# RWKV-7 time mixing in a two-layer hybrid: centred value rows, unsplit decay sums, the bonus moved to forward rounds, and another order between the states' steps

## Chip, cores and metric

The kernel runs on one core of one Trainium2 chip. The metric is the device time of one execution in microseconds (us); the time before is the median of three runs. Below, PE is TensorE (matmul), DVE is VectorE, ACT is ScalarE, POOL is GpSimd and SP is SyncE, which issues DMA transfers.

## What is computed

A backbone of two layers over 1024 latent tokens of width 1024, with 256 context tokens ahead. The first layer is attention; the second is bidirectional RWKV-7 time mixing beside a long convolution, and its output goes through a projection, a residual sum and a final norm. The change lies in the RWKV-7 part, eight heads of width 64, in two directions:

```python
def wkv_scan(s0, r, decay, k, v, kk, b, reverse, emit):
    def step(s, inp):
        r_t, w_t, k_t, v_t, kk_t, b_t = inp
        sa = jnp.einsum('bhij,bhj->bhi', s, kk_t)
        s = s * w_t[:, :, None, :] - sa[..., None] * b_t[:, :, None, :] + v_t[..., None] * k_t[:, :, None, :]
        y = jnp.einsum('bhij,bhj->bhi', s, r_t) if emit else None
        return s, y
...
def rwkv_readout(y, r, k_bonus, v, r_k, gn_w, gn_b):
    mean = jnp.mean(yf, axis=-1, keepdims=True)
    var = jnp.mean(jnp.square(yf - mean), axis=-1, keepdims=True)
    yn = ((yf - mean) * lax.rsqrt(var + RWKV_GN_EPS)).reshape(y.shape[:2] + (BRANCH_W,))
    yn = (yn * gn_w + gn_b).astype(v.dtype)
    bonus = jnp.sum(r * k_bonus * r_k, axis=-1, keepdims=True) * v
    return yn + bonus.reshape(yn.shape)
```

The readout's y is the sum over both directions. A row of the state has one value channel; y's mean over these channels is linear in the value rows.

## The kernel before

The scan is done in chunks. A **job** is a pair of heads j (four of them) in one direction d, forward (d = 0) before backward; a **unit** is 256 tokens of a job, the first of the five being the context (q = 0). So there are 8 x 5 = 40 units. `rwkv` runs nine of the units' first parts ahead, and then 45 rounds, `rw_round(b)` for b = -4 to 40. One round works on many units at different stages:

- `rw_next_load` and `rw_cast` (unit b + 14): the inputs of a front; the cast splits the decay logits `sg` into two parts `sgs` (ACT rounds, GpSimd takes the remainder) and makes `kd` and `af`.
- `rw_front` (unit b + 13): running sums of the decay, `cs_ps`, by products with a triangular matrix; exponentials on ACT; scaled keys `AKR`, `kd`, `BK` on DVE.
- `rw_turned`, `rw_gram` (the front of the round before): transposes (`bk_ps`), 16 small products `g_ps` of keys with keys, masked on DVE into `LG`; the diagonal 32x32 blocks go to DRAM (`LD`).
- `rw_invert`: for a whole job those blocks come back as `L` (80 blocks side by side, on 80 partitions), and 31 steps of forward substitution on DVE make their inverses X. A step is two instructions, tmp = L times X and X = X minus tmp. `PACE` says how many steps a round takes at each of three places: 2, 1 and 6. The first one is at the end of the round in which the job's last front is ready. The inverses go through DRAM (`XD`) to `XT`.
- `rw_keys_turned`, `rw_right` (unit b + 4): the right sides `rh_ps`, copied to R by ACT; `rw_first` (b + 3, `y_ps`), `rw_blocks`, `rw_second` (b + 2, `z_ps`, DVE takes it off R) and `rw_solved` (b + 1, `w_ps`): block substitution.
- `rw_trans` (b + 1): `ph_ps`, from which DVE makes PH and RT; `rw_own` (b + 1): the unit's own share `sy_ps` from UV.
- `rw_scan` (unit b): four steps, each PH times the state S, S again through ACT, and RT times S for the output.
- In a backward round with q > 0, `rw_bonus` loads six arrays and makes the bonus factor (GpSimd and DVE); a round later `rw_stats` subtracts the mean `gmu`, takes the variance `gvr` and scales Y, `rw_readout` does the bonus product `bo_ps`, the transposition `yt_ps`, the affine part and the gate, and `rw_split` splits the result for the projection.
- From round 28 on, `Final` loads, scales and splits the weights of the projection, and from round 31 projects row blocks (`fe_ps`) by the table `PLAN`, at the end of a round.

Inside the rounds PE, DVE, ACT and GpSimd keep the program's order (`nc.ordered(True)`); the order of SP's transfers is set by the scheduler. PSUM tiles of tag "f" share four banks in turn, so a product can wait until an older tile has been read: `rh_ps` comes to the bank of `z_ps`.

```python
for b in range(-4, 41):
    self.rw_round(b)
```

Of the kernel before, what the change touches and what calls it, by code (L numbers as in the profile page):

```python
# [29 lines left out]
def constants():  # L30
# [5 lines left out]
    c["k_ones2"] = b  # L36
    p = np.zeros((128, 128), np.float32)
# [90 lines left out]
PACE = (5, 2, 1, 6)  # L128
# [68 lines left out]
class K:  # L197
# [1064 lines left out]
    def rw_init(self):  # L1262
# [13 lines left out]
        tri = fp.tile([128, 3, 256], F32, name="tri0", tag="kkr", bufs=2)  # L1276
        nc.sync.dma_start(out=tri[:, 0:2], in_=a["k_tri"].rearrange("d p k -> p d k"))
        C["tri"] = fp.tile([128, 2, 256], F32R, name="tri", bufs=1)
        nc.vector.tensor_copy(out=C["tri"], in_=tri[:, 0:2])
# [38 lines left out]
    def rw_ready(self, n):  # L1318

        k, i, q = self.rw_unit(n)  # L1320
        cuts = INVS if k == 0 else (0, 5)
        if i + 1 in cuts:
            self.inv.append(self.rw_invert(self.fr[k], cuts[cuts.index(i + 1) - 1], i + 1))
            next(self.inv[0])

    def rw_whole(self):

        self.rw_cast(*self.rw_next_load())
# [11 lines left out]
    def rw_pre(self, sp):  # L1340
        nc, a = self.nc, self.a
        self.ones2 = sp.tile([128, 128], F32, name="ones2k")
        nc.sync.dma_start(out=self.ones2, in_=a["k_ones2"])
        self.e12 = sp.tile([128, 1], F32, name="e12")
        nc.vector.memset(self.e12, 1e-12)
# [74 lines left out]
    def rwkv(self):  # L1420
        nc, tc, a = self.nc, self.tc, self.a
        self.pst.close()
        with ExitStack() as st:
# [13 lines left out]
            while self.nf < 9:  # L1437
                self.rw_inv(PACE[0], True)
                self.rw_whole()
            self.rw_cast(*self.rw_next_load())  # L1440
            self.rw_inverses(0)
            self.rw_vectors(0)
            self.st2, self.late, self.last, self.whole, self.Y, self.F = ExitStack(), None, None, None, None, None
# [4 lines left out]
            self.F.after(41)  # L1448
# [4 lines left out]
    def rw_round(self, b):  # L1453
# [3 lines left out]
        step, bonus = [None] * 4, None  # L1457
        late, last, old = self.late, self.last, self.whole
        new = self.rw_next_load() if self.nl < 40 else None
        if at(b):  # L1460
            k, i, q = self.rw_unit(b)
            j, d = self.jobs[k]
            if i == 0 and d == 0:
                self.Y = self.wp.tile([128, 16, 64], F32, name="Y", bufs=2)
# [11 lines left out]
        if self.F:  # L1476
            self.F.split()
# [12 lines left out]
        self.rw_inv(PACE[1])  # L1490
# [35 lines left out]
        if late:  # L1526
# [5 lines left out]
        self.rw_inv(PACE[3])  # L1532

        if at(b + 1):
            self.rw_own(b + 1)
# [5 lines left out]
        if bonus:  # L1541
            self.late = (j, q, self.Y, *next(bonus))
        if b == 28:
            self.fpst.close()
            self.F = Final(self, self.st2)
        if b >= 28:
            self.F.after(b)
# [28 lines left out]
    def rw_cast(self, F, q):  # L1576
        G = F["g"][q]
        sgs = G["sgs"] = self.fp.tile([128, 2, 2, 128], F32R, name="sgs", bufs=2)
        self.split(sgs[:, 0], sgs[:, 1], G.pop("sg"))
        j = F["j"]  # L1580
        kd = G["kd"] = self.fp.tile([128, 256], F32, name="kd", bufs=2)
        self.nc.scalar.activation(out=kd, in_=G["af"], func=AF.Identity, scale=self.col("rwkv_k_a", j), bias=self.C["oka"][:, j:j + 1])
        self.nc.gpsimd.tensor_tensor(out=G["af"], in0=G["af"], in1=G["kkr"][:, 1], op=ALU.mult)

    def rw_front(self, F, q, wp, bufs):
# [5 lines left out]
        kkr, af, sgs, kd = (G.pop(n) for n in ("kkr", "af", "sgs", "kd"))  # L1591
# [18 lines left out]
        yield  # L1610
# [6 lines left out]
        kd = v3(kd)  # L1617
# [193 lines left out]
    def rw_own(self, n):  # L1811
# [4 lines left out]
        LG, BT, UV = (G.pop(t) for t in ("LG", "BT", "UV"))  # L1816
# [45 lines left out]
    def rw_bonus(self, j, q):  # L1862
# [11 lines left out]
        k, a0, a1, r, v, g = io  # L1874
        nc.gpsimd.tensor_tensor(out=a0, in0=a0, in1=a1, op=ALU.add)
# [488 lines left out]
```

## Time and profile before

| | us |
|---|---|
| median of three runs | 2593.4 (2593.35 to 2595.18) |
| profiled execution | 2604.29 |
| its span, first to last instruction | 2602.5 |
| PE busy / DVE / ACT / POOL | 2178.8 / 1561.3 / 1097.0 / 759.7 |
| mean granted PE clock | 0.900 |

The span holds the whole kernel. The rounds lie in its last quarter: round 0 begins at 1901.78 us and the last instruction ends at 2602.5. A round is counted here from the start of one DVE instruction, R minus z_ps, to the next. All durations below are of the one profiled execution.

### The profile page before, as it was taken

The page shows a single profiled execution, that of the slowest core. Times are in us where ns is not written, and L with a number is a line of the kernel's source. Part 1 is how long each engine was busy: PE and PEld are TensorE (multiplying, and loading weights), DVE is VectorE, ACT ScalarE, POOL GpSimd, SP SyncE. Part 2 cuts the span into 40 slices and gives each one's busy share as a digit, 9 for nine tenths or more (in the row PEclk, how much of TensorE's full clock was granted, in tenths as well). Part 3 has the DMA queues.
Part 4 walks back from the last instruction along what each step waited for, and adds up shares of the span by engine and source line. Part 5 has one row for each costly group of instructions (what it writes and reads, how often), then busy time and mean ns, then how long its engine had stood idle before and what let it go on. Part 6 is the DMA issues. An engine that isn't in the chain of part 4 may idle for free. (4 is left out here: it accounts for less than half of the span.)

```text
span 2602.5 us, 47059 instructions
## 1 busy us (share of the span) xinstructions
PE 2178.8 (84%) x17799; PEld 1831.3 (70%) x17799; DVE 1561.3 (60%) x3231; ACT 1097.0 (42%) x2307; POOL 759.7 (29%) x758
## 2 busy tenths in 40 slices
PE   5999999999999987888999899996476776756884
PEld 3877888777878875777787787884466665655763
DVE  6255522577687775554766864586767766665234
ACT  5354344556565555322322313752244444433223
POOL 1244245101114455211322442243112213122122
PEclk7999999999999888989999999997588787886987
DMA  8443355662125668344545445735334334344321
GB/s 269 132 126 106 124 165 168 201 215 82 58 72 174 190 183 223 130 168 146 157 125 170 156 137 184 264 106 148 88 89 111 98 89 114 97 130 123 89 79 71
DMA packets 351433, 361.80 MB, mean 139 GB/s; under 512 B 83106, under 2 KB 283055, under 8 KB 350438
## 3 DMA queue, kind: packets, MB, share of 16 engines
q1 hardware_dynamic: 341894, 330.34, 41.9%
q10 hardware_dynamic: 9168, 24.25, 3.0%
q0 software_dynamic: 144, 4.19, 0.4%
q8 instruction: 141, 2.31, 0.4%
q14 instruction: 86, 0.70, 0.1%
HBM read 260.07 MB, written 100.10 MB: 138 GB/s over the span
## 5 line engine op out<-in xcount | busy, mean ns | idle before, releaser
L157 PE MATMUL g_ps<-xl,w_hi 128*128 128x512 f32 x1056 | 269.7, 401 | 1.0 <-ACT w_hi L215 1.0
L157 PEld LDWEIGHTS g_ps<-xl,w_hi 128*128 128x128 f32 x1056 | 200.7, 192 | 44.8 <-issue 1.9
L157 PE MATMUL s_ps<-k,q 128*128 128x256 f32 (+1 forms) x704 | 200.4, 382 | 8.3 <-DVE pn L723 5.1
L219 DVE TENSOR_TENSOR w_lo<-w_raw,w_hi 128x256 fp32r<-128x256 f32 (+1 forms) x184 | 131.1, 768 | 89.0 <-ACT w_hi L215 42.7
L464 POOL TENSOR_TENSOR al_acc<-al_acc,al_t 128x512 f32<-128x512 f32 x98 | 128.8, 1314 | 186.7 <-ACT al_t L462 136.4
L210 ACT COPY pt<-pt_ps 128x512 f32<-128x512 f32 (+1 forms) x203 | 102.0, 506 | 140.1 <-PE pt_ps L160 134.3
L157 PE MATMUL sy_ps<-S,RT 64*64 64x64 f32 x512 | 51.9, 291 | 104.0 <-ACT S L175 104.0
L157 PE MATMUL g_ps<-xl,w_lo 128*128 128x512 f32 x528 | 138.3, 395 | 0.0
L160 PE MATMUL pt_ps<-ident,p 128*128 128x128 f32 x704 | 118.9, 285 | 16.1 <-DVE pt L208 7.1
L157 PE MATMUL g_ps<-xhi,w_hi 128*128 128x512 f32 (+1 forms) x528 | 118.5, 367 | 9.1 <-DVE ac_res L306 4.7
L157 PEld LDWEIGHTS s_ps<-k,q 128*128 128x128 f32 x704 | 110.4, 201 | 15.0 <-DVE p L723 6.7
L157 PEld LDWEIGHTS sy_ps<-S,RT 64*64 64x64 f32 x512 | 31.1, 166 | 124.4 <-ACT S L175 124.4
L718 ACT ACTIVATE p<-p,mn 128x1280 f32<-128x1280 f32 (+1 forms) x96 | 103.4, 1077 | 35.2 <-DVE p L723 35.1
L157 PE MATMUL g_ps<-xhi,w_lo 128*128 128x512 f32 (+1 forms) x528 | 118.2, 362 | 0.0
L160 PEld LDWEIGHTS pt_ps<-ident,p 128*128 128x128 f32 x704 | 81.5, 142 | 51.4 <-DVE pt L208 14.2
L157 PE MATMUL g_ps<-AKR,BK 64*64 64x128 f32 (+1 forms) x1280 | 72.5, 337 | 49.8 <-DVE AKR L1614 31.6
L175 DVE TENSOR_TENSOR tmp<-L,X 80x31 f32<-80x31 f32 (+15 forms) x217 | 83.5, 385 | 50.5 <-DMA L<-LD 45.8
L462 ACT ACTIVATE al_t<-al_w,condT 128x512 f32<-128x512 f32 x98 | 70.8, 722 | 100.3 <-POOL al_acc L464 63.1
L157 PE MATMUL g_ps<-xlo,w_hi 128*128 128x512 f32 (+1 forms) x528 | 113.0, 356 | 0.0
L157 PEld LDWEIGHTS g_ps<-xl,w_lo 128*128 128x128 f32 x528 | 98.2, 188 | 20.9 <-issue 1.4
L157 PEld LDWEIGHTS g_ps<-xhi,w_hi 128*128 128x128 f32 x528 | 90.3, 194 | 29.7 <-DVE qraw L572 5.6
L904 POOL TENSOR_TENSOR bias<-namask,tt 128x384 f32<-128x384 f32 x64 | 67.2, 1051 | 129.2 <-DVE mn L913 55.0
(421 smaller groups left out, 5751.0 us busy)
## 6 DMA issues: line engine op xcount, KB each, us to landing
w_raw<-rec_w_in SPq DMA_DIRECT2D x33, 512.0 KB
hfw<-FW SPq DMA_DIRECT2D x32, 512.0 KB
w_raw<-attn_w_in SPq DMA_DIRECT2D x13, 1024.0 KB
al_w<-rec_ada_w SPq DMA_DIRECT2D x48, 256.0 KB
tt<-TG SPq DMA_DIRECT2D x64, 192.0 KB
kkr<-KK SPq DMA_DIRECT2D x40, 256.0 KB
q<-qb SPq DMA_DIRECT2D x64, 128.0 KB
HS<-hs SPq DMA_DIRECT2D x32, 256.0 KB
```

The costliest lines, as they stand in the source:

```text
L157: return self.keep(self.pe.matmul(*args, **kw))
L160: return self.keep(self.pe.transpose(*args, **kw))
L175: ins = f(*args, **kw)
L210: self.nc.scalar.copy(out=out, in_=in_)
L219: e.tensor_tensor(out=lo, in0=full, in1=hi.bitcast(F32), op=ALU.subtract)
L462: nc.scalar.activation(out=o, in_=wt, func=AF.Copy, scale=self.condT[:, k, ci:ci + 1])
L464: nc.gpsimd.tensor_tensor(out=t, in0=t, in1=o, op=ALU.add)
L718: self.nc.scalar.activation(out=p, in_=p, func=AF.Exp, bias=mn, scale=-1.0, accum_out=rs)
L904: nc.gpsimd.tensor_tensor(out=b, in0=mask, in1=tt, op=ALU.subtract)
```

## The change

It touches the value rows, the front, the place of the bonus, and the order in a round.

- **Values.** The token-major value rows are made by a product with the matrix I - 1/64 per head (`cent`), where it was a transposition; y then has no mean, and `rw_stats` computes none.
- **Decay sums.** `tri` and `sg` stay in fp32: two products per front, not four of rounded parts. `rw_cast` is gone; `kd` and `af` are made in `rw_front`.
- **Bonus.** Loaded and computed in the forward round of the unit, on DVE and ACT, with its product in the same round; it is kept in `vg` until the backward round. The gate is loaded there.
- **GpSimd.** The gate's product and the remainders of splits go to DVE. It keeps af times kv and the variance's small instructions.
- **Order.** All 16 gram products lie before the second step, the own products between the second and third, the phi products before the fourth; the projection is a generator that gives six products at a time between the steps; `Final` starts at the head of round 28, not at its end. The loads of the next front are issued in the middle of the round.
- **Pace.** `AGES` replaces `PACE`: by rounds since a job's blocks are ready, 0 + 0 + 6 steps, twice 3 + 1 + 5, then 4 + 3 + the rest.

```diff
-PACE = (5, 2, 1, 6)
+PACE, AGES = 5, ((0, 0, 6), (3, 1, 5), (3, 1, 5), (4, 3, 99))
...
-                nc.tensor.transpose(ps[:, q, :], o[:, (t4 + q) * 128:(t4 + q + 1) * 128], self.ident)
+                nc.tensor.matmul(ps[:, q, :], o[:, (t4 + q) * 128:(t4 + q + 1) * 128], self.cent, start=True, stop=True)
...
+        if b == 28:
+            self.fpst.close()
+            self.F = Final(self, self.st2)
...
-            if d == 1 and q > 0:
-                bonus = self.rw_bonus(j, q)
-                next(bonus)
+            if q > 0:
+                if d == 0:
+                    bonus = self.rw_bonus(j, q)
+                    next(bonus)
+                else:
+                    g = self.wp.tile([128, 256], F32, name="iog", bufs=2)
+                    nc.sync.dma_start(out=g, in_=self.G1[j * 128:j * 128 + 128, q * 256 - 256:q * 256])
             step = self.rw_scan(b)
+        more = iter(())
+        if self.F:
+            more = self.F.round(b)
+            next(more)
...
         next(front, None)
-
-        if step[0]:
-            step[0]()
+        next(bonus, None)
+
+
+        step[0]()
         next(gram, None)
+        next(gram, None)
+        next(more, None)
         if old:
             self.rw_turned_out(*old)
         next(front, None)
-        if step[1]:
-            step[1]()
+        step[1]()
+        if at(b + 1):
+            self.rw_own(b + 1)
+        next(more, None)
+        self.rw_inv(pace[1])
         next(gram, None)
-        self.rw_inv(PACE[2])
-        next(gram, None)
-        if new:
-            self.rw_cast(*new)
-        if step[2]:
-            step[2]()
+        if self.nl < 40:
+            self.rw_next_load()
+        step[2]()
         if at(b + 4):
             self.rw_right(b + 4)
-        next(stats, None)
-        if step[3]:
-            step[3]()
         if at(b + 1):
             self.rw_trans(b + 1)
+        next(more, None)
+        next(stats, None)
+        step[3]()
+        v = next(bonus, None)
         if late:
             self.rw_readout(late)
...
-            for part in range(2):
-                nc.tensor.matmul(ps[:, i, :], sgs[:, part, i, :], C["tri"][:, d, :], start=(part == 0), stop=(part == 1))
+            nc.tensor.matmul(ps[:, i, :], sg[:, i, :], C["tri"][:, d, :], start=True, stop=True)
...
+        kd = fp.tile([128, 2, 128], F32, name="kd", bufs=1)
+        nc.scalar.activation(out=kd, in_=v3(af), func=AF.Identity, scale=self.col("rwkv_k_a", j), bias=C["oka"][:, j:j + 1])
+        nc.gpsimd.tensor_tensor(out=v3(af), in0=v3(af), in1=kv, op=ALU.mult)
+        yield
...
+        k, a0, a1, r, v = io
+        nc.vector.tensor_tensor(out=a0, in0=a0, in1=a1, op=ALU.add)
+        nc.scalar.activation(out=a0, in_=a0, func=AF.Identity, scale=C["hka"][:, j:j + 1], bias=C["oka"][:, j:j + 1])
+        nc.vector.scalar_tensor_tensor(out=r, in0=r, scalar=self.col("rwkv_r_k", j), in1=k, op0=ALU.mult, op1=ALU.mult)
+        nc.vector.tensor_tensor(out=a0, in0=a0, in1=r, op=ALU.mult)
+        yield
...
-        nc.vector.tensor_reduce(out=mu, in_=y, axis=AX.X, op=ALU.add)
-        nc.vector.tensor_scalar(out=mu, in0=mu, scalar1=-1.0 / 64, scalar2=None, op0=ALU.mult)
...
-        nc.vector.tensor_tensor(out=y, in0=y, in1=b16(mu), op=ALU.add)
...
-        nc.gpsimd.tensor_tensor(out=t, in0=t, in1=g, op=ALU.mult)
+        nc.vector.tensor_tensor(out=t, in0=t, in1=g, op=ALU.mult)
...
-            self.k.split(hi, lo, raw)
+            self.k.split(hi, lo, raw, lo_eng="v")
...
+                if n % 6 == 5 and n + 1 < len(terms):
+                    yield
```

In the order on PE, a round that has a front and a forward latent unit, before, from the decay sums to the third step's state product (S is the state, PH and RT the transition and read-out factors):

```order
L157 MATMUL cs_ps<-tri,sgs 128x256 x4
L157 MATMUL y_ps<-R,XT_17505 128x128 x4
L160 MATMUL bk_ps<-ident,BK 128x128 x4
L160 MATMUL rh_ps<-ident,AKR 128x2x64 x2
L157 MATMUL sy_ps<-S,PH 64x64 x2
L157 MATMUL sy_ps<-S,RT 64x64 x2
L157 MATMUL g_ps<-AKR,BK 64x128 x8
L157 MATMUL sy_ps<-S,PH 64x64 x2
L157 MATMUL sy_ps<-S,RT 64x64 x2
L157 MATMUL g_ps<-AKR,BK 64x128 x8
L157 MATMUL sy_ps<-S,PH 64x64 x2
```

And after, the same stretch of such a round and what follows it, up to the last step:

```order
L159 MATMUL cs_ps<-tri,sg 128x256 x2
...
L159 MATMUL g_ps<-AKR,BK 64x128 x16
L159 MATMUL sy_ps<-S,PH 64x64 x2
L159 MATMUL sy_ps<-S,RT 64x64 x2
L159 MATMUL sy_ps<-UV,BT 64x64 x2
...
L159 MATMUL rh_ps<-V,LG 64x64 x8
L159 MATMUL ph_ps<-BT,At 64x64 x4
L159 MATMUL ph_ps<-LG,At 64x64 x4
...
L159 MATMUL sy_ps<-S,PH 64x64 x2
L159 MATMUL sy_ps<-S,RT 64x64 x2
L159 MATMUL bo_ps<-ioa,ones_17498 64x256 x2
```

All gram products moved ahead of the second step, the own products (UV) from behind the last step to between the second and the third, the phi products from behind the last step to before it; in all four steps RT's product still stands right behind PH's.

In the order on DVE, a forward latent round after the change, at the keys of the front:

```order
L177 TENSOR_TENSOR AKR<-AKR,kkr 128x512
L177 TENSOR_TENSOR kd<-kd,kkr 128x256
L177 TENSOR_TENSOR ioa<-ioa,iob 128x256
L177 SCALAR_TENSOR_TENSOR ior<-ior,vec,iok 128x256
L177 TENSOR_TENSOR ioa<-ioa,ior 128x256
L177 TENSOR_TENSOR BK<-kd,E 128x2x128
L177 TENSOR_TENSOR BK<-af,E 128x2x2x64
L177 TENSOR_TENSOR tmp<-L,X 80x231
L177 TENSOR_TENSOR X<-X,tmp 80x11x21
L177 TENSOR_TENSOR LG<-g_ps,gm 128x512 x2
```

The three bonus instructions are new in this place, between the scaled key `kd` and `BK`; before, `BK` came right behind `kd`.

In the order on DVE after the change, where the projection's first weights are split:

```order
L177 TENSOR_TENSOR fLG<-fLG,fAKR 128x512
L177 TENSOR_TENSOR fw_23600<-fLG,fw_23598 128x512
L177 TENSOR_TENSOR fLG<-fLG,fBT 128x512
L177 TENSOR_TENSOR fw_23601<-fLG,fw_23599 128x512
L177 TENSOR_TENSOR fLG<-fLG,fAKR 128x512
L177 TENSOR_TENSOR fw_23604<-fLG,fw_23602 128x512
L177 TENSOR_TENSOR fLG<-fLG,fBT 128x512
L177 TENSOR_TENSOR fw_23605<-fLG,fw_23603 128x512
L177 TENSOR_TENSOR m_23808<-yo,m_23808 128x256
L177 TENSOR_TENSOR R<-R,z_ps 128x512
```

Each remainder (fw) moved from GpSimd to DVE, right behind the scaling (fLG) of the same weights, whose rounding by ACT lies between the two.

## Rows read from the trace of the kernel before

**Rows 1.** Windows by stage: length; busy us (instructions) of PE, PEld, DVE, ACT, POOL; clock.
```profile
1901.78:2051.31 149.53, 103.42 (x1622) 91.35 (x1616) 101.01 (x247) 61.61 (x176) 37.66 (x59) 0.80 0.37 101
2051.31:2207.18 155.87, 108.94 (x1756) 95.04 (x1756) 100.90 (x250) 67.78 (x195) 41.46 (x68) 0.78 0.38 103
2207.18:2319.30 112.12, 80.64 (x1386) 70.51 (x1386) 68.89 (x174) 50.71 (x144) 23.17 (x38) 0.85 0.36 97
2319.30:2342.55 23.25, 10.45 (x158) 9.01 (x158) 16.20 (x35) 7.94 (x20) 8.48 (x14) 0.65 0.64 180
```

**Rows 2.** Windows by round, rounds 10, 12, 14, 17, 18, 19; the same columns.
```profile
2051.31:2065.15 13.84, 11.23 (x178) 9.52 (x178) 12.82 (x33) 8.91 (x26) 5.69 (x9) 0.79 0.32 89
...
2078.87:2094.47 15.60, 10.36 (x194) 9.27 (x192) 4.54 (x11) 8.12 (x24) 2.45 (x4) 1.00 0.42 113
...
2108.30:2120.95 12.65, 9.30 (x155) 7.74 (x153) 12.10 (x28) 8.04 (x23) 1.59 (x2) 1.00 0.28 73
...
2147.06:2166.09 19.03, 11.27 (x214) 10.02 (x212) 7.68 (x21) 7.67 (x23) 7.33 (x15) 0.92 0.50 130
2166.09:2186.04 19.95, 12.35 (x198) 10.49 (x198) 14.43 (x37) 7.50 (x22) 7.27 (x13) 0.74 0.44 122
2186.04:2207.18 21.14, 13.84 (x166) 11.90 (x166) 16.30 (x36) 7.53 (x22) 8.19 (x13) 0.68 0.38 110
```

**Rows 3.** Waits, 1901.78 to 2367.68: total us, times, longest us.
```profile
PE sy_ps L157 <- ACT S L175: 75.3, 98, 12.7
...
PE rh_ps L160 <- DVE R L175: 46.5, 13, 6.3
```

**Rows 4.** Timeline of PE, round 12: start, us, instruction, [wait before and releaser].
```profile
2080.46 0.38 PE L160 MATMUL rh_ps<-ident,AKR 128*128 128x128 f32 x2
...
2081.58 0.27 PE L157 MATMUL sy_ps<-S,RT 64*64 64x64 f32 x2 [0.47 <-ACT S L175]
...
2085.90 0.27 PE L157 MATMUL sy_ps<-S,RT 64*64 64x64 f32 x2 [0.90 <-ACT S L175]
...
2089.52 0.71 PE L157 MATMUL cs_ps<-tri,sgs 128*128 128x256 f32 x4
2090.07 1.05 PE L157 MATMUL y_ps<-R,XT 128*128 128x128 f32 x8
...
2095.20 0.69 PE L160 MATMUL rh_ps<-ident,AKR 128*128 128x128 f32 x2 [3.64 <-DVE R L175]
```

**Rows 5.** Timeline of DVE: one subtraction in rounds 10 and 13, the inversion's first product.
```profile
2055.99 0.80 DVE L175 TENSOR_TENSOR X<-X,tmp 80x220 f32<-80x220 f32 x1
...
2094.14 0.19 DVE L175 TENSOR_TENSOR tmp<-L,X 80x31 f32<-80x31 f32 x1 [6.61 <-DMA L<-LD]
...
2108.00 0.38 DVE L175 TENSOR_TENSOR X<-X,tmp 80x220 f32<-80x220 f32 x1
```

**Rows 6.** Timeline of DVE: the mean's subtraction in rounds 27 and 28, a weight's scaling.
```profile
2318.96 0.42 DVE L175 TENSOR_TENSOR Y<-Y,gmu 128x256 f32<-128x256 f32 x1
...
2337.52 0.68 DVE L175 TENSOR_TENSOR fLG<-fLG,fAKR 128x512 f32<-128x512 f32 x1
...
2341.19 1.44 DVE L175 TENSOR_TENSOR Y<-Y,gmu 128x256 f32<-128x256 f32 x1
```

**Rows 7.** Groups by line and shape from 1780 us on: busy us, mean ns.
```profile
L175 DVE SCALAR_TENSOR_TENSOR ioa<-ioa,vec,ior 128x256 f32<-128x256 f32 x16 | 7.6, 477 | 9.5 <-POOL ioa L175 9.5
...
L175 POOL TENSOR_TENSOR af<-af,kkr 128x256 f32<-128x256 f32 x30 | 24.5, 818 | 0.7 <-ACT kd L175 0.7
```

**Rows 8.** Timeline of SP's queue in round 12: four issues of LD.
```profile
2087.08 1.84 SPq L1668 DMA_DIRECT2D LD<-LG  x4
```

**Rows 9.** Timelines of POOL and ACT in round 28: the weights' split.
```profile
2338.93 6.20 POOL L175 TENSOR_TENSOR fw<-fLG,fw 128x512 fp32r<-128x512 f32 x4 [4.34 <-ACT fw L175]
...
2338.23 2.42 ACT L175 CAST fw<-fLG 128x512 fp32r<-128x512 f32 x4 [4.87 <-DVE fLG L175]
```

**Rows 10.** Timeline of PE near the end: the last transposition of Y.
```profile
2574.19 1.12 PE L157 MATMUL yt_ps<-ident,Y 64*64 64x64 f32 x16 [8.05 <-DVE Y L175]
```

More of the change, by code (lines that the diff above doesn't have):

```diff
@@ L1437, in rwkv @@
             while self.nf < 9:
-                self.rw_inv(PACE[0], True)
+                self.rw_inv(PACE, True)
                 self.rw_whole()
-            self.rw_cast(*self.rw_next_load())
+            self.rw_next_load()
             self.rw_inverses(0)
             self.rw_vectors(0)
-            self.st2, self.late, self.last, self.whole, self.Y, self.F = ExitStack(), None, None, None, None, None
+            self.st2, self.late, self.last, self.whole, self.F, self.age = ExitStack(), None, None, None, None, 0
             nc.ordered(True)
@@ L1447, in rwkv @@
             self.rw_split(self.last)
-            self.F.after(41)
+            for _ in self.F.round(41):
+                pass
             nc.ordered(False)
@@ L1456, in rw_round @@
         at = lambda n: 0 <= n < 40
-        step, bonus = [None] * 4, None
+        step, bonus = [lambda: None] * 4, iter(())
         late, last, old = self.late, self.last, self.whole
-        new = self.rw_next_load() if self.nl < 40 else None
+        pace = AGES[min(self.age, 3)]
+        self.age += 1
+        if b == 28:
+            self.fpst.close()
+            self.F = Final(self, self.st2)
         if at(b):
@@ L1531, in rw_round @@
             self.rw_outputs(b)
-        self.rw_inv(PACE[3])
-        if at(b + 1):
-            self.rw_own(b + 1)
+        self.rw_inv(pace[2])
+        for _ in more:
+            pass
         if old:
@@ L1540, in rw_round @@
         self.last, self.late = late, None
[L1541 to L1547, printed above, removed]
+        if at(b) and q > 0:
+            if d == 0:
+                self.vg[q] = v
+            else:
+                t = self.wp.tile([128, 256], F32, name="yo", bufs=2)
+                self.late = (j, q, self.Y, self.vg[q], g, t)
     def rps(self, shape, name, tag="f"):
@@ L1590, in rw_front @@
         G = F["g"][q]
-        kkr, af, sgs, kd = (G.pop(n) for n in ("kkr", "af", "sgs", "kd"))
+        kkr, af, sg = (G.pop(n) for n in ("kkr", "af", "sg"))
         K0 = math.exp(-0.5)
@@ L1908, in rw_stats @@
         yield
-        nc.vector.tensor_tensor(out=y, in0=y, in1=b16(vr), op=ALU.mult)
+        nc.vector.tensor_tensor(out=y, in0=y, in1=vr.unsqueeze(2).to_broadcast([128, 4, 64]), op=ALU.mult)
         yield
     def rw_readout(self, late):
-        nc, wp = self.nc, self.wp
-        j, q, Y, v, g, a0 = late
-        ps = self.rps([128, 256], "bo_ps")
+        nc = self.nc
+        j, q, Y, v, g, t = late
         pt = self.rps([128, 4, 64], "yt_ps")
-        for h in range(2):
-            zo = slice(64 * h, 64 * h + 64)
-            nc.tensor.matmul(ps[zo], self.C["ones2"][zo, zo], a0[zo], start=True, stop=True, tile_position=(64 * h, 64 * h))
         for ci in range(4):
@@ L1934, in rw_split @@
         j, q, _, _, _, t = late
-        if j == 3:
-            m = self.m3[q]
-            self.split(m[:, 0], m[:, 1], t)
-            return
-        m = [wp.tile([128, 256], F32R, name="m1", tag="m1", bufs=2) for _ in range(2)]
-        self.split(m[0], m[1], t)
-        for p in range(2):
-            nc.sync.dma_start(out=self.M1[p, j * 128:j * 128 + 128, q * 256 - 256:q * 256], in_=m[p].bitcast(F32))
+        m = self.m3[q] if j == 3 else wp.tile([128, 2, 256], F32R, name="m1", tag="m1", bufs=1)
+        self.split(m[:, 0], m[:, 1], t, lo_eng="v")
+        if j < 3:
+            for p in range(2):
+                nc.sync.dma_start(out=self.M1[p, j * 128:j * 128 + 128, q * 256 - 256:q * 256], in_=m[:, p].bitcast(F32))
     def reduced_sin(self, out, ps, bias, pool):
@@ L2290, in norm, with round @@
             nc.sync.dma_start(out=self.a["out"][t * 128:t * 128 + 128, self.cs[h]], in_=x[h])
-    def after(self, b):
+    def round(self, b):
         nc, k, take = self.nc, self.k, self.take
         ep, wp = k.ep, k.wp
+        self.split()
         four = lambda f: [[f(i, h) for h in range(2)] for i in range(2)]
@@ L2327, in after @@
                 self.fetch(*items[n + 1][:2])
-            self.project(t, ks, last)
+            yield from self.project(t, ks, last)
         if later:
```

69 lines of the change are left out of this document (28 added, 41 removed).

## The prediction, made before the changed kernel ran

> **What bounds the kernel now.** I read the windows view first, cut where DVE starts to take z_ps off R, which it does once in each round. [Rows 1] is the table by stage: the first ten rounds take 149.53 us, the next ten 155.87, the next eight 112.12, and round 28 alone 23.25. In the 155.87 us TensorE is busy 108.94, DVE 100.90, GpSimd 41.46: no engine is full. Then I cut that stage into rounds [rows 2], of which six of the ten are shown. Rounds 10 and 14 are DVE's (12.82 busy of 13.84, 12.10 of 12.65); rounds 17 to 19 take 19 to 21 us, of which TensorE is busy 11 to 14, at mean granted clocks of 0.92, 0.74 and 0.68 (1.00 is the 2.4 GHz level, and what lies between is a mean with the 1.2 GHz one). Third, the waits of rounds 0 to 29 [rows 3]: TensorE waits 46.5 us in 13 waits for R on DVE, and 75.3 us in 98 for the state S on ACT, one of them 12.7 us. Last, the timelines. [Rows 4] is a round without a disturbance and its end: the second product of a step waits 0.47, that of the last step 0.90, and the next round's rh_ps waits 3.64 for R. [Rows 5] says why: DVE works in program order; it stood 6.61 us at the job's first inversion product, until L had come, and took R after that. So a round costs the longest of four: TensorE's products with the steps' waits, DVE's row of work, the way of LG through DRAM to L, or ACT and GpSimd where they stand ahead of S.
>
> **What each part costs.** A difference of 0.2%, 5 us, is about what a measurement here can tell from none.
>
> *Waits in the steps.* RT's product still comes right behind PH's, so the 0.47 stays in all four steps. Only the last step gains: the phi products now lie ahead of it and the R copy on ACT is done, 0.90 - 0.47 = 0.43 a round [rows 4].
>
> *Decay sums.* Four products of the split values become two of fp32. Bounds: the 0.71 of the four now, and the 1.05 of y_ps, which has as many columns in fp32 [rows 4]. I take the upper one, +0.3 on TensorE in each round with a front. The cast and the remainder that go were beside other work: 0.
>
> *Centred values.* The readout of a backward round loses a sum, a short scaling and a subtraction on DVE. The subtraction takes 0.42 alone and 1.44 beside GpSimd [rows 6]; with the sum, of the same size, the three are 1.0 to 2.5. They stand ahead of R in DVE's order and count in full, 1.0 to 1.3 in most of 16 rounds. Ahead of the loop 40 transpositions become products with a matrix, as long or up to 0.1 longer, beside other engines' work: 0, with +4 kept for the range.
>
> *Bonus.* Backward rounds lose a product of 0.477 [rows 7], iov times bo_ps and the bonus product on TensorE; forward rounds get these and two more like the 0.42 row [rows 6], about 1.7 on DVE, and 0.4 on TensorE (between nothing and the 1.05 of y_ps; two products of 256 columns on half arrays, so nearer to nothing). Round 14 is DVE's and shows it: +0.95 after 0.7 for fewer collisions with GpSimd, and so I take for 15. In round 12, where DVE waits for L, it is free.
>
> *GpSimd.* The same 80x220 subtraction takes 0.80 beside a GpSimd instruction and 0.38 without [rows 5]. GpSimd is busy 7.3 to 8.2 us in rounds 17 to 19 [rows 2]; at 0.818 for one [rows 7] that is nine instructions, of which a half to all lengthen one of DVE's by 0.42: 2 to 3 us in such a round, 0.8 in round 10, and nearly all go. One per front stays, af times kv, now beside DVE's work on the keys. At the 0.42 it costs what it costs now. By a rule of the Trainium skill ("SBUF — State Buffer", section "Who interferes with whom") a DVE instruction with two SBUF inputs and a GpSimd one that reads SBUF shut each other out for the whole instruction. The trace shows half of it, 0.42 of 0.818. By the rule the one that stays would cost 0.4 more in 27 rounds, and my sum would end 11 us later, inside the range.
>
> *The way of L.* All gram products now lie ahead of the second step, and the loads for the next front are asked for in mid-round, behind LD instead of ahead of it. LD was asked for at 2087.08 [rows 8] and L had landed by 2094.14 [rows 5], 15 us behind the round's R; I put it at 12. Rounds 12 and 17 live on this: 15.60 to 12.3 and 19.03 to 13.0, where the mean's chain followed the wait.
>
> *Pacing.* A job's inversion makes nine steps a round as now, but none ahead of the states' steps in its first round, so its larger ones come later: +0.8 in round 10. There the work on yt_ps also falls behind the last step: +0.9, and 0.42 for the gate's product, which GpSimd did.
>
> So the ten rounds come to 15.0, 14.0, 12.3, 13.0, 13.6, 12.6, 12.5, 13.0, 15.0 and 16.5, together 137.5: **-18.4**. Rounds 18 and 19 lose the mean's 1.0 to 1.3, the 0.477, 0.42, 2 to 3 of collisions and 0.43, and get 0.42 for the gate. Rounds 0 to 9 are the same work, 137.5 again: **-12**. Rounds 20 to 27 at the same rates are 103: **-9**.
>
> *Rounds 28 and 29.* The projection's weights are scaled and split here. GpSimd takes 6.20 for four remainders, and ACT's casts wait 4.87 for DVE [rows 9]; the variance stands behind the one and S behind the other, which makes the 12.7 [rows 3]. Now the remainders are DVE's, and each stands behind its own cast: 0.68 to scale [rows 6], 0.6 for the cast (a fourth of 2.42 [rows 9]), 0.68, with hand-overs 2.1, four times 8.4 ahead of R, where 2.4 of scaling and 2.6 of the mean's chain with collisions stand now: +3.4. Against it: the variance no longer waits for GpSimd (-1.4), six inversion products without collisions (-2.4), 0.477, 0.43. I take **-2** for both rounds together.
>
> *The rest.* Round 30 -1.5, for its variance; the mean's chain in the last backward rounds -4; at the end TensorE waits 8.05 for Y before yt_ps [rows 10], where groups of the projection now come first and the mean is gone, -5; 0.43 in five rounds -2; further weight splits on DVE +1.5. Together **-11**.
>
> Sum: -12 - 18.4 - 9 - 2 - 11 = -52.4. The profiled execution took 2604.3, so 2551.9 is for one like it. The median of the runs stands 10.9 lower, at 2593.4: **2541**.
>
> **Rivals.**
>
> B, *the clock stays up.* In round 12 TensorE had the full clock, and from rh_ps to the next without its wait is 2095.20 - 3.64 - 2080.46 = 11.1 us [rows 4]; with -0.43 + 0.3 + 0.4 it is 11.4. Rounds 18 and 19, behind waits of several us, ran at 0.74 and 0.68. If with the waits the low clocks go, 28 rounds come to 12.3 on average, DVE's rounds among them, instead of 13.75: -41, so 2500. For it: rounds 12 and 14 at 1.00. Against: rounds that DVE bounds leave TensorE idle still. 16%.
>
> C, *SyncE is full.* A forward round asks for 21 transfers, where it was 16; four take 1.84 [rows 8], so 21 need 9.7 us, and more where the queue stands: a bonus load waits until its buffer is free, which for one of them is the last round's bo_ps, and LD stands behind it. If that bounds those rounds, 5 x 0.46 = 2.3 in 16 of them: +37, 2578. For it: L is waited for already. Against: only job starts need L. The Trainium skill ("DMA: Bandwidth & Descriptors", section "Issuing engines are not separate DMA queues") speaks against it too: the time to start a transfer is usually small beside the transfer itself. In the trace a start takes 0.46. 14%.
>
> D, *slower.* The bonus stands on DVE between the keys' product and BK. If its loads land after DVE has come there, BK waits, and with it the gram products, LG and L. The place is 16 forward rounds: the gain is gone at 52.4 / 16 = 3.3 us of waiting in each, and the kernel is slower by over 0.2% from 3.6. At the 6.61 that L cost, it would be 16 x 6.61 = 106: 2647. For it: the loads of a round reuse the buffers of the round before. Against: a load asked for at 2090.43 had landed by 2094.14, in 3.7, and DVE gets to the bonus a third into the round. 6%.
>
> E, *nothing comes of it*: DVE's work hardly falls in number, and R comes as late by another wait; 2593. 4%.
>
> **How the numbers follow.** 60% for the forecast; its own range is 2515 to 2565 (28 rounds, each 0.9 to either side, and the 4 of the centred values). B lies with two thirds of its chance above 2492, C with half of its below 2575. Left out are about 5% below, and above it 7% of C, D and E: 2492 to 2575. Faster are the forecast, B, C and a little of E, 0.91; slower is D, 0.06; same 0.03.
>
> **What would show it.** Right: rounds 17 to 19 at 13 to 17 us, no wait for L over 3 us, GpSimd under 2 us busy in a round, the 80x220 subtraction at 0.38 everywhere, rounds 14 and 15 a little longer, and in rounds 28 and 29 DVE's scalings and remainders in turn with waits for ACT. Wrong: a granted clock near 1.00 through whole stages (B); SyncE without a gap in forward rounds, with L late (C); DVE waiting at ioa or ior (D); rounds as long as now, with another releaser of R (E).

## The result, and the profile after

The changed kernel takes **2640.1 us** (median of four runs, 2630.6 to 2642.1), against 2593.4 before: a ratio of 1.0172, 95% interval 1.0147 to 1.0197. It is slower by 47 us; 2541 was forecast. The profiled execution took 2642.1, with a span of 2640.1.

The windows by stage of the changed kernel answer to [rows 1] (same columns); stages are cut at the same instruction:

```profile
1897.74:2054.55 156.81, 115.69 (x1644) 99.16 (x1636) 98.44 (x249) 64.32 (x180) 14.42 (x28) 0.76 0.36 98
2054.55:2212.19 157.64, 115.33 (x1756) 99.70 (x1756) 100.37 (x254) 67.44 (x189) 18.75 (x34) 0.82 0.37 102
2212.19:2339.97 127.78, 93.68 (x1392) 80.95 (x1392) 75.79 (x190) 50.47 (x139) 11.65 (x21) 0.77 0.35 95
2339.97:2365.76 25.79, 12.63 (x154) 11.26 (x154) 12.07 (x31) 7.89 (x20) 0.98 (x5) 0.61 0.55 165
...
2405.01:2535.38 130.37, 103.78 (x973) 80.02 (x974) 40.52 (x82) 30.62 (x80) 0.00 (x0) 0.88 0.30 87
```

The last line is rounds 31 to 36, which took this before:

```profile
2382.84:2494.66 111.82, 97.16 (x948) 81.71 (x950) 28.22 (x55) 27.54 (x75) 12.47 (x12) 0.86 0.33 94
```

Each of these stages got longer, by 7.3, 1.8, 15.7, 2.5 and 18.6 us, although GpSimd's busy time is about half of what it was or less. The windows by round, rounds 10, 12, 14 and 17 to 19, answer to [rows 2]:

```profile
2054.55:2070.18 15.63, 10.67 (x167) 9.84 (x168) 13.14 (x34) 6.09 (x18) 3.57 (x6) 0.78 0.28 82
...
2089.75:2104.49 14.74, 11.45 (x186) 9.94 (x185) 6.65 (x16) 6.59 (x18) 2.00 (x3) 0.88 0.53 148
...
2121.05:2140.16 19.11, 12.89 (x151) 10.79 (x150) 12.87 (x32) 6.52 (x18) 0.72 (x1) 0.64 0.29 80
...
2160.19:2179.72 19.53, 12.91 (x204) 11.19 (x203) 7.20 (x18) 8.06 (x24) 3.12 (x8) 0.91 0.45 116
2179.72:2195.26 15.54, 11.17 (x208) 9.38 (x206) 9.36 (x28) 8.19 (x24) 2.63 (x6) 1.00 0.44 119
2195.26:2212.19 16.93, 12.65 (x158) 11.24 (x158) 13.40 (x33) 7.23 (x21) 3.29 (x6) 0.70 0.33 97
```

The backward rounds 18 and 19 fell from 19.95 and 21.14 to 15.54 and 16.93, as forecast. The forward round 14 rose from 12.65 to 19.11, and its clock fell from 1.00 to 0.64. So the loss of the first thirty rounds lies in forward rounds. The waits of rounds 0 to 29 answer to [rows 3]:

```profile
PE sy_ps L159 <- ACT S L177: 100.8, 96, 11.6
...
ACT ioa L177 <- DVE ioa L177: 33.4, 12, 6.8
...
DVE tmp L177 <- DMA L<-LD: 10.4, 6, 4.4
```

DVE's row for L was this before:

```profile
DVE tmp L175 <- DMA L<-LD: 35.7, 6, 7.4
```

TensorE's wait for R nearly went (46.5 to 3.3 us), DVE's wait for L fell from 35.7 to 10.4 us, but S on ACT rose from 75.3 to 100.8, and there is a new row: ACT waits for DVE's `ioa`. The timelines of round 14 show where, PE before and after the change first, then ACT and DVE after it:

```profile
2110.21 0.27 PE L157 MATMUL sy_ps<-S,RT 64*64 64x64 f32 x2 [0.48 <-ACT S L175]
```

```profile
2122.15 0.33 PE L159 MATMUL sy_ps<-S,PH 64*64 64x64 f32 x4
2126.67 0.37 PE L159 MATMUL sy_ps<-S,RT 64*64 64x64 f32 x2 [4.19 <-ACT S L177]
```

```profile
2121.38 0.56 ACT L177 COPY Z<-y_ps 128x512 f32<-128x512 f32 x1
2125.82 0.60 ACT L177 ACTIVATE ioa<-ioa,oka,hka 128x256 f32<-128x256 f32 x1 [3.88 <-DVE ioa L177]
2126.33 0.29 ACT L177 ACTIVATE S<-sy_ps,Dt 128x64 f32<-128x64 f32 x1
```

```profile
2121.05 0.68 DVE L177 TENSOR_TENSOR R<-R,z_ps 128x512 f32<-128x512 f32 x1
...
2125.03 0.42 DVE L177 TENSOR_TENSOR kd<-kd,kkr 128x256 f32<-128x256 f32 x1
2125.37 0.42 DVE L177 TENSOR_TENSOR ioa<-ioa,iob 128x256 f32<-128x256 f32 x1
```

PE's first state product is done at 2122.5. ACT could make S then, but the bonus scale stands ahead of S in its order and waits for DVE's sum, which stands behind R, three inversion steps and the keys. PE waits 4.19 us at the first step, where the same wait was 0.48 before. Over the 16 forward latent rounds this one wait adds up to 57.6 us in the timelines, against 9.1 before (the expectation of run 1 has 10.2, which is 1.1 too high).

### The profile page after: what moved, and what is told of

It is laid out like the page before. It is cut to its first block, busy times and chain, and to the rows that moved or that the text cites. A ratio compares the mean times of both kernels' runs of the same rounds, so it can differ in the third digit from the quotient of the medians.

```text
span 2640.1 us, 46983 instructions
## 1 busy us (share of the span) xinstructions
PE 2228.0 (84%) x17839; PEld 1857.2 (70%) x17839; DVE 1558.7 (59%) x3263; ACT 1088.9 (41%) x2279; POOL 645.2 (24%) x606
## 3 DMA queue, kind: packets, MB, share of 16 engines
q0 software_dynamic: 144, 4.19, 0.4%
## 5 line engine op out<-in xcount | busy, mean ns | idle before, releaser
L177 ACT ACTIVATE S<-sy_ps,Dt 128x64 f32<-128x64 f32 x160 | 49.8, 311 | 183.4 <-PE sy_ps L159 183.3
L159 PEld LDWEIGHTS s_ps<-k,q 128*128 128x128 f32 x704 | 109.2, 198 | 15.3 <-DVE p L725 7.3
L159 PEld LDWEIGHTS g_ps<-xl,w_lo 128*128 128x128 f32 x528 | 98.6, 188 | 20.7 <-issue 0.7
L159 PEld LDWEIGHTS g_ps<-xhi,w_lo 128*128 128x128 f32 x528 | 89.8, 191 | 18.9 <-issue 5.8
L177 POOL TENSOR_TENSOR af<-af,kkr 128x256 f32<-128x256 f32 x31 | 26.1, 843 | 311.5 <-ACT kd L177 257.4
```

The lines of the kernel that those rows point to most:

```text
L159: return self.keep(self.pe.matmul(*args, **kw))
L177: ins = f(*args, **kw)
```

## The experiments

Ratios are to the kernel before, run beside each on the same chip. In these sets its medians were 2599 to 2601 us, so 0.1% is 2.6 us.

**1. ACT's bonus scale made by DVE.**

```diff
-        nc.scalar.activation(out=a0, in_=a0, func=AF.Identity, scale=C["hka"][:, j:j + 1], bias=C["oka"][:, j:j + 1])
+        nc.vector.tensor_scalar(out=a0, in0=a0, scalar1=C["hka"][:, j:j + 1], scalar2=C["oka"][:, j:j + 1], op0=ALU.mult, op1=ALU.add)
```

> The changed kernel with the bonus scale (a = a * k_a/2 + 1 - k_a) made by DVE in the same place of the program, where ACT makes it; nothing else is changed. Theory A: ACT keeps program order, its scale stands ahead of the state S of the first step and waits there for DVE's first bonus sum, which stands behind R, the inversion steps and the keys; in the 16 forward latent rounds the first step's wait on PE sums to 57.6 us, where it was 10.2 before. By A the waits at the first step fall to about 0.5 to 0.9, the time falls by 40 to 60 us less 16 x 0.4 us more of DVE: 2575 to 2605 us, and no clear difference or a gain against the kernel before. Rival N (it is the new order of the products that makes the rounds long, the wait only shows who came last): the wait moves to another releaser and the time stays at 2620 to 2640 us.

Measured: 1.0000 (0.9982 to 1.0018). One instruction on another engine takes back the whole loss, some 45 us by the ratios (39 by the medians). Round 14 is 14.12 us long, and the first step's wait there is short again:

```profile
2110.39 0.27 PE L159 MATMUL sy_ps<-S,RT 64*64 64x64 f32 x2 [0.47 <-ACT S L177]
```

**2. The bonus group behind the second step.** `next(bonus)` moves from ahead of `step[0]()` to behind `step[1]()`, with the scale on ACT.

> The changed kernel with the whole bonus group (three DVE instructions and ACT's scale) resumed behind the second step and not ahead of the first. Theory A: 2570 to 2600 us, as in the run with DVE's scale or somewhat better, since the three instructions then also stand behind BK on DVE; if DVE comes to them later than ACT to its scale, a smaller wait appears at the third step in rounds with many inversion steps (1 to 2 us in four or five rounds per pair of heads) and the time is 2590 to 2615. Rival N: 2620 to 2640.

Measured: 1.0008 (0.9995 to 1.0021), the same as by DVE's scale. ACT still waits for DVE's `ioa`, 20.7 us in seven long waits, but S of the first two steps is no longer behind it. Both runs bear out theory A.

**3. The bonus alone, on the kernel before.** `rw_bonus` of the changed kernel in forward rounds, the gate loaded in backward rounds, and nothing else.

> The kernel before with one part of the change alone: the bonus moved to the forward rounds, on DVE and ACT, its group ahead of the first step, the product behind the last. Theory A: slower than before by 25 to 55 us (first-step waits of 2 to 6 us in 16 rounds, less about 10 us for what leaves the backward rounds): 2618 to 2648 us. Rival N: within 10 us of before, 2585 to 2603.

Measured: 1.0104 (1.0083 to 1.0124), 27 us slower, with the same new wait in its list:

```profile
ACT ioa L175 <- DVE ioa L175: 41.3, 13, 7.4
```

So the move alone makes the old kernel slower, in the old order of products too, although it takes the bonus off GpSimd and out of the backward rounds (18 and 19 take 17.54 and 18.67 us here, 19.95 and 21.14 before). Rival N falls.

**4. The projection's products at the end of a round**, in run 1's kernel (three of the four `next(more, None)` taken out).

> The changed kernel with DVE's scale and all products of the projection at the end of a round, as before the change, instead of six at a time between the steps. Theory A: within 8 us of the run with DVE's scale alone, since the same products are done by the same engine. Rival N for the last stage (rounds 31 to 36 took 130.4 us where they took 111.8): 10 to 20 us less than the run with DVE's scale alone.

Measured: 1.0020 (1.0007 to 1.0033), 5 us from run 1 with intervals that overlap. Where the products lie hardly matters; the 18.6 us that rounds 31 to 36 lost have another cause, and 10.5 of them are already gone in run 1, with the scale on DVE (119.91 us).

With the coupling gone the kernel is only as fast as before, and 52 us of the forecast are still missing. The next runs look for them.

**5. The remainders of the projection's weights on GpSimd again**, in run 1's kernel: `self.k.split(hi, lo, raw)` without `lo_eng="v"`.

> The run with DVE's scale, and the remainders of the projection's weights on GpSimd again. Theory D (each remainder on DVE waits for its own cast, which holds DVE ahead of R in rounds 28 and 29, and ACT's casts hold S, 6.57 us in round 33): rounds 28 and 29 go from 25.8 + 24.9 to 44 to 48 us together, the first-step wait of round 33 from 6.6 to about 2, and the time falls by 5 to 12 us against the run with DVE's scale: 2588 to 2598. Rival (GpSimd holds the variance as long as DVE held R): rounds 28 and 29 as now, within 4 us.

Measured: 0.9954 (0.9938 to 0.9970), 12 us less than run 1. In the changed kernel's timeline of DVE in round 28 each remainder stands behind its own cast:

```profile
2356.76 0.68 DVE L177 TENSOR_TENSOR fLG<-fLG,fAKR 128x512 f32<-128x512 f32 x1
2358.12 0.69 DVE L177 TENSOR_TENSOR fw<-fLG,fw 128x512 fp32r<-128x512 f32 x1 [0.68 <-ACT fw L177]
2358.73 0.68 DVE L177 TENSOR_TENSOR fLG<-fLG,fBT 128x512 f32<-128x512 f32 x1
2360.10 0.69 DVE L177 TENSOR_TENSOR fw<-fLG,fw 128x512 fp32r<-128x512 f32 x1 [0.68 <-ACT fw L177]
```

A pair takes 1.97 us, four of them 7.9 ahead of R. With GpSimd, rounds 28 and 29 are 21.26 and 22.47, not 25.79 and 24.93, and the first step's wait of round 33 falls from 6.57 to 3.52, less than theory D said. Rounds 31 to 36 come back to what they took before the change (111.82), run 1 first, then this run:

```profile
2379.91:2499.82 119.91, 98.05 (x965) 75.54 (x964) 41.95 (x86) 28.27 (x75) 0.00 (x0) 0.93 0.34 97
```

```profile
2362.65:2473.84 111.19, 96.05 (x965) 74.52 (x964) 39.94 (x77) 28.24 (x75) 11.00 (x8) 0.95 0.35 102
```

Theory D stands. Of what the last stage lost, 10.5 us were the bonus scale's and 8.7 the remainders'.

**6. The old pace** of 2 + 1 + 6 steps, in run 1's kernel (`AGES` with four times (2, 1, 6)).

> The run with DVE's scale, and the inversion at the old pace (2 + 1 + 6 steps in every round). Theory P (the new pace lays the last seven steps into the round whose products wait for XT): waits for XT of 4.3 to 5.3 us six times fall to 2 to 3, the round behind them is 3 to 5 us shorter, and the time falls by 8 to 20 us. Rival X (the way X - DRAM - XT is what counts and its end hardly moves, since the last step stays in the same round; and rounds 13 to 15 carry three more steps): within 8 us of the run with DVE's scale, XT waits as they are.

Measured: 1.0011 (0.9991 to 1.0031). Theory P falls by the time, though not by its wait. Two waits of run 1, then the same of this run:

```profile
PE y_ps L159 <- DMA XT<-XD: 29.7, 7, 5.3
DVE tmp L177 <- DMA L<-LD: 22.0, 7, 9.3
```

```profile
DVE tmp L177 <- DMA L<-LD: 33.2, 6, 8.4
PE y_ps L159 <- DMA XT<-XD: 10.3, 4, 3.6
```

The waits for XT fell as P said, and DVE's waits for L rose by 11.2 us: what is not waited for in one place is waited for in another.

**7. The inversion's end a round earlier**, in run 1's kernel.

```diff
-AGES = 5, ((0, 0, 6), (3, 1, 5), (3, 1, 5), (4, 3, 99))
+AGES = 5, ((2, 1, 6), (3, 1, 6), (3, 1, 7), (4, 3, 99))
```

> The run with DVE's scale, and the inversion's 31 steps done within three rounds (1, 9, 10, 11), a round earlier. Theory X (the rounds that got short, 7.8 and 10.2 us, run ahead into the way of X through DRAM: PE waits 4.3 to 5.3 us for XT six times, and its clock then stays low for a whole round, so that rounds 12, 17 and 22 take 22 us): no XT wait over 1 us, rounds 12, 17 and 22 at 13 to 17 us; DVE's rounds pay 1 to 2 us each in three rounds of five; the time falls by 15 to 35 us: 2566 to 2586. Rival (DVE's row bounds the rounds on average, and what is not waited for in one round is waited for in another): within 8 us of the run with DVE's scale.

Measured: 1.0013 (0.9995 to 1.0031). The rival holds. In run 1, round 12 had waited for XT and then run at a low clock (timeline of PE, the window of the round with a mean clock of 0.63, and two parts of it):

```profile
2077.66 1.51 PE L159 MATMUL y_ps<-R,XT 128*128 128x128 f32 x8 [4.51 <-DMA XT<-XD]
```

```profile
2072.32:2095.08 22.76, 16.34 (x183) 13.85 (x182) 7.53 (x16) 6.41 (x18) 2.03 (x3) 0.63 0.47 119
```

```profile
2073.20:2077.60 4.40, 0.00 (x0) 0.00 (x0) 2.43 (x4) 1.33 (x4) 2.03 (x3) 1.00 0.35 71
...
2079.00:2094.00 15.00, 13.09 (x168) 11.01 (x167) 3.30 (x9) 4.43 (x12) 0.00 (x0) 0.50 0.51 135
```

The clock was still 1.00 while TensorE waited, and 0.50, the 1.2 GHz level, in the 15 us behind it. In run 7 that wait is gone and another one stands in its place, in DVE's timeline of the same round, which still takes 21.39 us:

```profile
2089.43 0.19 DVE L177 TENSOR_TENSOR tmp<-L,X 80x31 f32<-80x31 f32 x1 [10.81 <-DMA L<-LD]
```

The round before had become short (9.05), so DVE came to the first inversion product that much before L did. L also came late for another reason. DVE had finished LG at 2077.64, but in SP's queue LD was asked for 4.4 us later, behind seven loads, three of them the bonus's (`iok`, `ioa`, `iob`):

```profile
2076.36 1.28 DVE L177 TENSOR_TENSOR LG<-g_ps,gm 128x512 f32<-128x512 f32 x2
```

```profile
2077.41 0.38 SPq L1586 DMA_DIRECT2D sg<-SG  x1
...
2082.08 1.80 SPq L1680 DMA_DIRECT2D LD<-LG  x4
...
2085.43 0.46 SPq L1724 DMA_DIRECT2D L<-LD  x1
```

In the changed kernel itself LD had followed LG at once in this round (2096.78 and 2096.81). No run moved these loads, so what their place costs is not shown.

**8. Centred values alone, on the kernel before.**

> The kernel before with one part of the change alone: the value rows centred by the product with I - 1/64, and no mean in the readout. By the prediction's term, 1.0 to 1.3 us for most of 16 rounds and more where GpSimd collides: 12 to 25 us faster than before. Rival (the readout's instructions lie in DVE's idle time, since R waits for z_ps or L anyway): within 6 us of before.

Measured: 1.0018 (1.0001 to 1.0035): no gain, if anything 5 us lost. The lines by shape from 1600 to 1690 us show the price ahead of the loop, changed kernel first, then before:

```profile
L159 PE MATMUL vt_ps<-cent,rwo 128*128 128x128 f32 x80 | 12.3, 275 | 0.4 <-DVE rwo L1144 0.4
```

```profile
L160 PE MATMUL vt_ps<-ident,rwo 128*128 128x128 f32 x40 | 7.0, 274 | 0.7 <-DVE rwo L1142 0.7
```

A transposition is one record of 0.275 us, a product in fp32 two. The records overlap, so the 40 more of them add 5.3 us of busy time (12.3 for 7.0), where PE is the bound. From the first of them to the first decay sum, before and changed:

```profile
1607.70:1762.90 155.20, 152.80 (x753) 125.54 (x752) 106.35 (x113) 95.15 (x170) 55.53 (x50) 1.00 0.57 187
```

```profile
1605.90:1772.10 166.20, 163.01 (x819) 135.62 (x818) 108.62 (x114) 90.95 (x166) 59.00 (x49) 1.00 0.54 177
```

The stretch is 11.0 us longer. The other half of that is in the groups by shape of these two windows, before and changed:

```profile
L157 PE MATMUL g_ps<-xl,w_hi 128*128 128x512 f32 x320 | 82.9, 399 | 0.0
L157 PE MATMUL g_ps<-xl,w_lo 128*128 128x512 f32 x157 | 43.6, 402 | 0.0
```

```profile
L159 PE MATMUL g_ps<-xl,w_hi 128*128 128x512 f32 x336 | 86.9, 400 | 0.0
L159 PE MATMUL g_ps<-xl,w_lo 128*128 128x512 f32 x166 | 45.1, 397 | 0.0
```

The whole program has the same number of these products in both kernels (1056 and 528 records), but 25 more of them, 5.5 us, now lie ahead of the first decay sum. In this run the stretch is as long, 165.9 us, with 28 of them moved. From the first R on the kernel saves 5.7 us (717.1 against 722.8 to the end of the span).

**9. The inversion's first step a round later**, with DVE's scale and GpSimd's remainders. L is loaded when the job's last front is ready, the first product comes in the next round.

```diff
+        if q1 - q0 == 5:
+            yield
         for s in (range(31) if d == 0 else range(31, 0, -1)):
...
+AGES = 5, ((0, 1, 7), (3, 1, 6), (3, 1, 6), (4, 3, 99))
```

> DVE's scale, remainders on GpSimd, and the inversion's first step taken out of the round in which the job's last front is ready: L is only loaded there, and its 31 steps follow as 8, 10, 10 and 3 in the next rounds. Theory L (the long rounds 12, 17 and 22 are made by DVE standing at the first inversion product until LG has gone through DRAM to L, ahead of R; earlier endings of the inversion only move the wait there): no wait of DVE for L, rounds 12 and 22 at 14 to 18 us where the run without this had 19.7 and 22.6; 10 to 20 us less than the run with the remainders on GpSimd: 2569 to 2579. Rival X (the way X to XT takes over): waits for XT of 4 to 5 us stay, rounds 12, 17 and 22 stay near 20, and the time changes by less than 6 us.

Measured: 0.9860 (0.9833 to 0.9887), 24 us less than run 5 by the ratios, which are from two chips; between the two profiled executions it is 17.2 us from round 0 to the end. Theory L holds. DVE's waits for L in run 5 and in this run:

```profile
DVE tmp L177 <- DMA L<-LD: 19.5, 6, 8.3
```

```profile
DVE tmp L177 <- DMA L<-LD: 2.7, 1, 2.7
```

Rounds 12 and 13 of this run:

```profile
2068.47:2080.03 11.56, 9.63 (x183) 8.29 (x182) 7.00 (x14) 6.10 (x18) 2.04 (x3) 1.00 0.51 141
2080.03:2095.07 15.04, 12.19 (x208) 10.32 (x206) 10.93 (x30) 9.16 (x26) 1.80 (x2) 1.00 0.52 138
```

Round 12 takes 11.56 us at full clock, where run 5 had 19.65, at full clock too, with 8.28 us of waiting for L. TensorE's waits for XT remain in three rounds, 11.6 us, so rounds 7, 17 and 27 still take 18 to 21.

**10. The values not centred**, in run 5's kernel: the transposition, and the mean in the readout.

> DVE's scale, remainders on GpSimd, and the value rows transposed as before the change, with the mean taken in the readout again. In the traces the 40 products with the centring matrix keep PE busy 22.0 us where the transpositions took 10.9, in a stretch in which PE has no idle time to hide them. Theory V: 11 us less ahead of the loop, 5 to 8 us more in the backward rounds: 3 to 8 us less than the run with the remainders on GpSimd. Rival (the 11 us are hidden): 5 to 10 us more than that run.

Measured: 0.9978 (0.9965 to 0.9990), 6 us more than run 5, with intervals that touch. Theory V was right on the 11 us ahead of the loop (153.0 from the first value product to the first decay sum, 164.8 in run 5), though not on why: its 22.0 and 10.9 us are sums of records that overlap, and the products are busy 12.3 and 7.0. The means cost more in the loop than it said: from the first R to the end 726.1 in this trace, 704.4 in run 5's. These two executions lie 15.6 us apart, the medians only 5. With the 10.5 us that are saved from the first value product to the first R, the medians put the means at some 16 us in the loop, the traces at 21.7.

**11. The first step later, on the kernel before** (the same `yield`, and `PACE` with 2 + 1 + 7).

> The kernel before with one thing alone that the change did not have: the inversion's first step is not taken in the round in which the job's last front is ready (L is only loaded there), and a round makes ten steps, not nine. Theory L (in program order the first product holds R of the same round until L is there; 35.7 us of such waits in six rounds before): rounds 2, 7, 12, 17, 22 and 27 lose 3 to 7 us each, and the time 15 to 30 us: 2570 to 2585. Rival (XT then comes later and is waited for instead, or the tenth step costs it again): within 8 us of before.

Measured: 0.9957 (0.9941 to 0.9973), 11 us less: below theory L's 15 to 30, and more than the rival's 8. DVE's waits for L fall to 7.6 us in three, and the six rounds that theory L names lose 31.6 us together, as it said. Much of it comes back: rounds 4, 14 and 24 take 2.9 to 3.2 us more each, rounds 6 and 26 take 3.0 and 7.2 more, and PE's waits for R stay (48.7 us in 13).

**12. Run 9's kernel with the values centred by DVE** as they leave PSUM.

```diff
-                nc.tensor.matmul(ps[:, q, :], o[:, (t4 + q) * 128:(t4 + q + 1) * 128], self.cent, start=True, stop=True)
+                nc.tensor.transpose(ps[:, q, :], o[:, (t4 + q) * 128:(t4 + q + 1) * 128], self.ident)
...
+            nc.vector.tensor_reduce(out=mu[:, 0:m], in_=pv, axis=AX.X, op=ALU.add)
+            nc.vector.tensor_scalar(out=mu[:, 0:m], in0=mu[:, 0:m], scalar1=1.0 / 64, scalar2=None, op0=ALU.mult)
+            nc.vector.tensor_tensor(out=vt[:, t4:t4 + m, :].rearrange("p t (h f) -> p t h f", f=64), in0=pv,
+                                    in1=mu[:, 0:m].unsqueeze(3).to_broadcast([128, m, 2, 64]), op=ALU.subtract)
```

> The run with the inversion's first step a round later, and the value rows transposed as before the change, their mean over a head's 64 columns taken off by DVE as they leave PSUM (a sum, a scaling and a subtraction per four tiles, in place of a copy that DVE and ACT shared), so that the readout still needs no mean. Theory V (PE bounds the stretch ahead of the loop, and the centring products cost 11 us there, while each mean in the readout costs more than 1 us in the loop): 6 to 11 us less than the run without this, 2555 to 2560. Rival (DVE becomes late with the values): no change or some us more.

Measured: **0.9804** (0.9768 to 0.9840), 2548.2 us (2546.4 to 2559.2) beside 2600.7: faster than both kernels, and 15 us under run 9 by the ratios, which are again from two chips. From the first value product to the end the two traces differ by 11.5 us; another 12.8 lie ahead of it, where the two programs are the same. So theory V's 6 to 11 is about what its part gave. The stretch ahead of the loop is back at 154.0 us.

```profile
1598.10:1752.10 154.00, 152.38 (x752) 125.62 (x750) 112.77 (x143) 91.22 (x162) 53.65 (x48) 1.00 0.57 187
```

DVE is busy 112.77 us in it, 6.4 more than in the kernel before, beside a PE that bounds it. That 2548 lies near the forecast 2541 does not bear the forecast out: in this kernel the scale, the remainders, the centring and the inversion's start are all other than in the changed one.

## Why the prediction was wrong, point by point

- **Bonus: the step that failed.** It was priced on DVE (1.7) and TensorE (0.4), and its ACT instruction, the scale, had no price at all. The prediction named the bound, "ACT and GpSimd where they stand ahead of S", and did not apply it to this instruction. What it cost is what stood behind it: S of the first step. Runs 1, 2 and 3 show it, 35 to 45 us in the new kernel (by the medians or the ratios of runs 1 and 2) and 27 in the old one. Rival D had the place and the rounds, and a gain that was gone at 3.3 us of waiting in each of 16; the added wait was (57.6 - 9.1) / 16 = 3.0. But D looked for late loads and for BK, and gave it 6%. The order on ACT was not read next to those on PE and DVE.
- **The way of L.** "Rounds 12 and 17 live on this": 12.3 and 13.0 were forecast. The term that was mis-sized is the 12 us from the round's R to L: it was 15.3 before, 14.4 after the change, and 21.6 and 21.1 in runs 1 and 7. From asking for LD to L's first use took 7.1 to 7.5 us in all four. L comes no sooner relative to the round before it either; a shorter round 11 only lets DVE come to it earlier (run 7: 10.81 us of waiting, behind a round of 9.05). In run 1, with the coupling gone, rounds 12 and 17 took 22.76 and 21.75. Run 9 shows that the time was there to be had, by starting the inversion a round later, not by an earlier L.
- **Centred values.** Ahead of the loop 0 was taken, 4 at most; it was 11.0, as PE had almost no idle time there: 5.3 for the products, and as much for other products that came to lie ahead of the first decay sum. In the loop 16 to 20 were taken; the old kernel gave 5.7 (run 8), the new one 16 to 22 (run 10, by the medians or the traces).
- **Rounds 28 and 29.** The pairs of scaling and remainder were foreseen at 2.1 each (1.97 measured), but the sum gave -2 for these rounds, where it became +2.3, and later splits +1.5; run 5 puts all of the remainders at 12. In "the rest", -11 in the sum, rounds 31 to 36 alone became +18.6, by the scale and the remainders.
- **Decay sums.** +0.3 a front was right: 1.03 for the two, 0.71 before. That the casts and GpSimd's remainders were worth nothing in the loop was not tried by itself. Ahead of it the stretch from the first decay sum to the first R fell from 116.8 to 106.7; it is neither the values (116.9 in run 8) nor the bonus (117.5 in run 3), and which other part it is stays open.
- **Last step's wait**: 0.90 to 0.43 to 0.50, as forecast. **GpSimd**: busy 18.75, not 41.46, in rounds 10 to 19, but up to 3.57 in a round where under 2 was the sign. Rounds 18 and 19 came out within 0.6 us of the forecast 15.0 and 16.5. Most of their 4.2 to 4.4 us has a run: 1.0 to 1.3 without the mean (run 8: 18.66 and 20.14), as forecast, and 2.4 to 2.5 by the bonus's move, which took it off GpSimd (run 3). The part of GpSimd's collisions was not tried by itself.
- **Rivals.** B fell: the clock of the middle stage is 0.82 (0.78 before), and round 18 at 1.00 is followed by round 19 at 0.70. C fell as a bound on every forward round: rounds 13 and 14, with 21 transfers, came down to 13.4 and 14.1 us in run 1. But its sign, a full queue with L late, stands in round 12 of run 7, where LD waited 4.4 us for its turn. The Trainium skill ("DMA: Bandwidth & Descriptors", section "Issuing engines are not separate DMA queues") says that the time to start a transfer is usually small beside the transfer itself. The trace agrees for one transfer (0.46 to start L, 4.0 until it was used), but the starts ahead of LD added up to 4.4 us, 1.69 of it for one (`iok`). E's time did not come about, but run 1, with the coupling gone, takes what E forecast, the time before, and DVE's busy time in rounds 10 to 19 hardly fell, as E said (100.90 to 100.37).

Still open: the waits for XT behind the short rounds 6, 16 and 26 (11.1 us in three in run 12), TensorE's longest wait for S around rounds 29 and 30 (11 to 15 us in all versions), and a new one, DVE waiting for the bonus load `ior`, 16.2 us in four in run 12, which is rival D's mechanism in shorter rounds.

## What to carry to other kernels

When work moves, list for each in-order engine what now stands behind each moved instruction, also the shortest one: 0.6 us of ACT that needed DVE's late result held the recurrence on PE. A wait on data that goes through DRAM was cured here by using the data a round later, not by making the round before it shorter. And an instruction is free only in the stretch in which it runs: the centring was cheap on DVE, and on PE, which was busy 152.8 of 155.2 us there, it made the stretch 11 us longer.

## What had not been expected of the hardware

An fp32 product of 128x128 shows as two records of 0.275 us, the transposition of the same tile as one. A product with the identity that is made by the product's instruction shows as two as well: the eight of `yt_ps` are 16 records in [rows 10]. The records overlap, so their durations must not be added up: 80 were busy for 12.3 us, 40 for 7.0. And one wait of 4.5 us costs more than itself: behind it TensorE's clock was 0.50 for 15 us, in which it was busy 13.09. In the whole round it was busy 16.34 us, where run 9 did the same round's work in 9.63 at 1.00.
